# Where the weights begin in their tiles: 144 bytes in, not 192 and 0

## The chip, the cores and the metric

The kernel runs on one core of one Trainium2 chip. The metric is the device time of one execution in microseconds. Before the change it is 1110.81 us, the median of three runs (1109.86 to 1111.26).

## What is computed

One decoder layer on 512 tokens of width 1024, in float32: a feed-forward network (FFN), a token mixer, a second FFN, each with an RMS norm before it and behind it and added back to the tokens. Cut to what the change touches:

```
D_MODEL = 1024; SEQ = 512
D_FF = ((8 * D_MODEL // 3 + 127) // 128) * 128        # 2816

def swiglu(x, w_gate, w_up, w_down):
    return (jax.nn.silu(x @ w_gate) * (x @ w_up)) @ w_down

h = rms_norm(x, ffn1_pre[l])
x = x + 0.5 * rms_norm(swiglu(h, ffn1_w_gate[l], ffn1_w_up[l], ffn1_w_down[l]), ffn1_post[l])
h = rms_norm(x, mix_pre[l])
y = token_mixer(h, w_in[l], ...)
x = x + rms_norm(y, mix_post[l])
h = rms_norm(x, ffn2_pre[l])
x = x + 0.5 * rms_norm(swiglu(h, ffn2_w_gate[l], ffn2_w_up[l], ffn2_w_down[l]), ffn2_post[l])
```

The change concerns `x @ w_gate` and `x @ w_up` of both FFNs.

## The kernel before

**Three matmuls for one product.** Every float32 operand is split into a rounded high half (`fp32r`) and the rest, the low half. ScalarE writes the high half (a copy that rounds, line 384), VectorE the low half (a subtraction, line 391). `mm3` (lines 413 to 415) then multiplies high by high, high by low and low by high, and adds the three in PSUM. With weights on the left they are the stationary operand: each of the three matmuls has its own load of 128 columns of weights, and the tokens, transposed (`xh`, `xl`), are the moving operand. In the profile's names `pb_F<-xh_t,whi` is a matmul that moves `xh` past the weights `whi`.

**The weights' tiles.** `wpair` takes a tile `whi` and a tile `wlo`, each [128, 1088] in float32, three buffers of each. The pair of a split uses 1024 of the 1088 columns, from column `shift` on: byte 4 x `shift` of the tile on every partition. `wsplit` takes such a pair and fills it.

**Two ways of multiplying gate and up.** A *unit* is 128 columns of one of the two weight matrices: 8 weight tiles of 128 x 128 (one for each 128 of the 1024 rows), so 24 matmuls, each of 512 columns of tokens. At the start of each FFN, when only half of the tokens are normalised, four units are multiplied in two halves: 24 matmuls of 256 columns on the first half of the tokens, and 24 later on the second. Of the four the first three take their weights from `wpair`; the fourth has its weights in four other buffers (`wslots`, tag `SP`). Units that are not halved, and these three before the change, have `shift` 0.

Most of the columns are not done by units but by *block products* (`strassen`): the product of a block of two rows and two columns (gate and up together, two column blocks of 128 each) is formed from 7 products instead of 8. Each of the 7 is 4 weight tiles by 2 column halves, 3 matmuls each: 24 matmuls of 256 columns. Its weights, often a sum or a difference of raw weight blocks, are split by `block`, which has a `shift` of `SHIFT` = 48 columns, 192 bytes. One call of `strassen` (a *pair*: 7 products, 168 matmuls) covers 256 columns of gate and of up. The first FFN has 9 such calls (`p` from 2 to 10), the second 10 (`p` from 1 to 10); the rest of the 11 are units.

In the first FFN each call also carries VectorE work for later: sums and differences on the down weights (`weight_sums`, `early_sums`, `down_sums`, line 762), which go through HBM. At the beginning of each FFN sums on the tokens (`token_sums`) ride along as well.

**The order.** The order of the instructions on TensorE, ScalarE and VectorE is written out as a list of numbers (`ORDER`) and laid on the program at the end. DMAs are issued by SyncE. PSUM banks have the names `pb_S`, `pb_T`, `pb_V`, `pb_F`.

**Elsewhere in the mixer** a projection (`proj_T`) multiplies weights from `wsplit` with shift 0 by halves of the tokens too, 256 columns a matmul. The diff doesn't touch it.

Of the kernel before, what the change touches and what calls it, by code (L numbers as in the profile page):

```python
# [22 lines left out]
P = 128  # L23
D = 1024
S = 512
KT = D // P
# [268 lines left out]
            8: ["of"] * 2 + ["V"] * 2, 9: ["KB"] * 4}  # L295
STEPS = (2, 2, 2), (4, 2)
EARLY = 5
SHIFT = 48
HOLD_TAGS = ["W"] * 2 + ["Q"] * 4 + ["KA"] * 2 + ["V"] * 2 + ["CB", "ring"]
PS_BUFS = dict(S=3, T=2, V=1, F=2)  # L300
PS_TAGS = [t for t in PS_BUFS for _ in range(PS_BUFS[t])]
# [7 lines left out]
class Layer:  # L309
# [264 lines left out]
    def ffn(self, n, wg, wu, wd, post, finish, xsrc, tags, nps, aside=None):  # L574
# [7 lines left out]
        raws = {}  # L582
        first = {}

        def unit(m, f, slots=False):
            w = {"g": wg, "u": wu}[m]
            if self.pre_split:
                return self.pre_split.pop(0)
            if f % 2 == 0:
                raws[m] = self.raw(w[:, f * P:(f + 2) * P].rearrange("(k p) f -> p k f", p=P), [KT, 2 * P])  # L590
            src = raws[m][:, :, (f % 2) * P:(f % 2 + 1) * P]
            if slots:
                return self.wslots(src, "SP", (self.last_cast, self.last_update) if n else None)
            return self.ktiles(self.wsplit(src, [KT, P]))

        def mms(w, b, lo, hi):
            c = slice(lo, hi)
            for k in range(KT):
                self.mm3(b[:, c], w[0][k], w[1][k], self.xh[k][:, c], self.xl[k][:, c], lo + k == 0, k == KT - 1, lo > 0)
# [12 lines left out]
        def block(src):  # L612

            return self.wsplit(src, [4, 2 * P], None, SHIFT)

# [68 lines left out]

        todo = [(m, f) for f in range(NF) for m in "gu"]
        for tag, (m, f) in zip(tags, todo):
            w = unit(m, f, len(first) == 3)
            b = self.bank(tag)
            first[m, f] = w, b
            mms(w, b, 0, 2 * P)  # L690
            if len(first) in (2, 3) and self.pending:
                self.pending.pop(0)()
# [5 lines left out]
        def classical(f, act):  # L698
            bs = []
            for m in "gu":  # L700
                if (m, f) in first:
                    w, b = first[m, f]
                    mms(w, b, 2 * P, S)
                else:
                    w = unit(m, f)
                    b = self.bank()
                    mms(w, b, 0, S)
                bs.append(b)
            nc.scalar.activation(act, bs[0], AF.Silu)
            nc.vector.tensor_mul(act, act, bs[1])  # L710
            g = f - 1 + n
            if g == 0:
                sums.extend(self.token_sums())
            if 0 <= g < len(STEPS[n]):
                with self.behind(self.last_rest):
                    for _ in range(STEPS[n][g]):
                        sums.pop(0)()

        c = slice(0, H), slice(H, S)
        for p in range(NF // 2):  # L720
# [26 lines left out]
            hi, lo = [self.slot(tags["E"].pop(0), F32R) for _ in range(2)]  # L747
# [1021 lines left out]
    def run(self, out):  # L1769
        nc, a = self.nc, self.a  # L1770
        self.xdram = self.tc.dram_tile([S, D], F32, name="xdram")
        self.x2dram = self.tc.dram_tile([S, D], F32, name="x2dram")
        self.tdram = self.tc.dram_tile([NF // 2, P, 4, S], F32, name="tdram")
        self.odram = self.tc.dram_tile([NF // 2, P, S], F32, name="odram")
        self.x = [self.slot("x") for _ in range(2 * NT)]

        def lx(t):
            for h in range(2):
                nc.sync.dma_start(self.x[2 * t + h], a["x"][0][t * P:(t + 1) * P, h * S:(h + 1) * S])

        ET = mybir.EngineType
        w1 = {"g": a["ffn1_w_gate"][0], "u": a["ffn1_w_up"][0]}
        self.pre_raw = {n: self.tile(self.pool, [P, KT, 2 * P], F32, "raw", "raw", 3) for n in "gu"}

        def lw(n, i, k0=0, k1=KT):
            c = slice(i * P, (i + 1) * P)
            nc.sync.dma_start(self.pre_raw[n][:, k0:k1, c],
                              w1[n][k0 * P:k1 * P, c].rearrange("(k p) f -> p k f", p=P))

        lx(0)  # L1790
        lx(1)
        self.new_xT()
        idle = self.bank("V")

        def keep_busy(n):

            for i in range(n):
                nc.tensor.transpose(idle[:, (i % 4) * P:(i % 4 + 1) * P], self.ident, self.ident)

        with nullcontext() if ORDER else self.tc.manual_schedule(engines={ET.Activation, ET.DVE, ET.PE}):  # L1800
            keep_busy(BUSY[0])
            g = self.row_spread(a["ffn1_pre"][0], "FF")
            keep_busy(BUSY[1])
            junk = self.pre_raw["g"].rearrange("p k f -> p (k f)")[:, 0:S // 2].bitcast(BF16)
            sq = self.meansq(self.x[0], S, 1.0, junk)
            lw("g", 0, 0, 4)
            lw("g", 0, 4, KT)
            lx(2)
            lw("u", 0)
            lx(3)  # L1810
            lw("g", 1)
            lw("u", 1)
            sq0 = [sq, self.meansq(self.x[1], S)]
            sq1 = self.squares(1)
            r0 = self.rstd(sq0)
            scale0, transpose0, cast0, rest0, _ = self.norm_steps(0, g, OPEN[0])
            scale1, transpose1, cast1, rest1, _ = self.norm_steps(1, g, OPEN[1])
            hi, lo = self.wpair([KT, P])
            src = self.pre_raw["g"][:, :, 0:P]

            def whi(k):
                nc.scalar.copy(hi[:, k:k + 4], src[:, k:k + 4])

            def wlo(k):
                nc.vector.tensor_sub(lo[:, k:k + 4], src[:, k:k + 4], hi[:, k:k + 4].bitcast(F32))

            for h in range(2):
                scale0(h, r0)
                transpose0(h)
            keep_busy(BUSY[2])  # L1830
            r1 = self.rstd(sq1)
            cast0(0)
            scale1(0, r1)
            transpose1(0)
            rest0(0)
            whi(0)
            cast0(1)
            scale1(1, r1)
            keep_busy(BUSY[3])
            transpose1(1)  # L1840
            wlo(0)
            cast1(0)
            rest1(0)
            keep_busy(BUSY[4])
            whi(4)
            rest0(1)
            wlo(4)
            cast1(1)
            rest1(1)
            self.pre_split = [self.ktiles(w) for w in ((hi, lo), self.wsplit(self.pre_raw["u"][:, :, 0:P], [KT, P]))]  # L1850
            sq2 = self.squares(2)
            t2 = self.norm_T(2, g, OPEN[2], sq2, whole=True)
            self.pre_split.append(self.ktiles(self.wsplit(self.pre_raw["g"][:, :, P:2 * P], [KT, P])))
            sq3 = self.squares(3)
            r3 = self.rstd(sq3)
            self.pre_split.append(self.wslots(self.pre_raw["u"][:, :, P:2 * P], "SP"))
            t3 = self.norm_T(3, g, OPEN[3], r=r3, whole=True)
        self.pending = [t2, t3]

        def boundary(post, pre, store, tags=None, whole=False):  # L1860
            def load():
                return self.gains((post, pre))

            def finish(t, gain, r=None):
                if store is not None:
                    for h in range(2):
                        nc.sync.dma_start(store[t * P:(t + 1) * P, h * S:(h + 1) * S], self.x[2 * t + h])
                if pre is not None:
                    if t == 0:
                        self.new_xT()  # L1870
                    self.pending.append(self.norm_T(t, gain, tags[t], r=r, whole=whole))
            return load, finish

        self.ffn(0, a["ffn1_w_gate"][0], a["ffn1_w_up"][0], a["ffn1_w_down"][0],
                 *boundary(a["ffn1_post"][0], a["mix_pre"][0], self.xdram, AFTER_FFN), a["x"][0], "TTSV", 6, self.distances)
        self.mixer(*boundary(a["mix_post"][0], a["ffn2_pre"][0], self.x2dram, AFTER_MIX, True))
        self.ffn(1, a["ffn2_w_gate"][0], a["ffn2_w_up"][0], a["ffn2_w_down"][0],
                 *boundary(a["ffn2_post"][0], None, out), self.x2dram, "TTFS", 3)
# [31 lines left out]
```

## Time and profile before

| | |
|---|---|
| median of three runs | 1110.81 us (1109.86 to 1111.26) |
| the profiled execution | 1109.86 us, its span 1107.8 us |
| granted TensorE clock, mean | 0.999 |
| TensorE matmuls busy | 1098.6 us (99%), 7070 matmuls |
| weight loads busy | 996.2 us (90%) |
| VectorE busy | 915.5 us (83%) |
| ScalarE busy | 654.2 us (59%) |
| block products, first FFN | 59.4 to 237.4 us |
| block products, second FFN | 799.1 to 996.5 us |

How it is read: a matmul's drawn duration is that of its way through the array, in which the next ones already follow. What a matmul costs in a dense stretch is the distance from its start to the next one's start. The timeline gives starts (first column, us from the begin of the span) and durations (second column, us); weight loads have a row of engines of their own, `PEld`. The windows view gives, for a stretch, the busy time of each engine and the count of its instructions.

### The profile page before, as it was taken

How to read it: one execution, taken by the hardware profiler on the slowest of the kernel's cores; microseconds unless marked ns; L12 is line 12 of the kernel's file. 1: busy time of each engine (PE TensorE's matmuls, PEld its weight loads, DVE VectorE, ACT ScalarE, POOL GpSimd, SP SyncE). 2: the span in 40 equal slices, each digit the busy share in tenths (PEclk: the TensorE clock that was granted, in tenths of full speed). 3: DMA queues.
4: the chain of work that ended last, by engine and by line, in shares of the span. 5: the costliest groups of instructions: out<-in, count | busy, mean ns of one | idle time of the engine just before them, and what ended most of it. 6: DMA issues, size and time to landing. Idle time of an engine off the chain costs nothing.

```text
span 1107.8 us, 18832 instructions
## 1 busy us (share of the span) xinstructions
PE 1098.6 (99%) x7070; PEld 996.2 (90%) x7070; DVE 915.5 (83%) x1569; ACT 654.2 (59%) x1185; POOL 79.1 (7%) x112
## 2 busy tenths in 40 slices
PE   9999999999999999999999999999999999999997
PEld 7899999998889988888888998888999999998886
DVE  7799999988787878987666687977898888979674
ACT  6455555566564778787565625645565555558562
POOL 1000000000012022443000000001000000000001
PEclk9999999999999999999999999999999999999999
DMA  9967775788964562202567768683324434267862
GB/s 293 308 199 245 225 228 181 222 289 281 317 203 119 165 168 86 84 22 62 169 217 252 236 181 294 220 292 105 103 89 129 129 122 130 92 196 232 294 221 83
DMA packets 153951, 207.36 MB, mean 187 GB/s; under 512 B 19938, under 2 KB 98562, under 8 KB 153604
## 3 DMA queue, kind: packets, MB, share of 16 engines
q1 hardware_dynamic: 153856, 206.16, 57.5%
q8 instruction: 55, 0.90, 0.3%
q14 instruction: 36, 0.29, 0.1%
q10 hardware_dynamic: 4, 0.00, 0.0%
HBM read 166.76 MB, written 39.37 MB: 186 GB/s over the span
## 4 chain that ended last, share of the span: by engine, by line
PE 92%; DVE 3%; DMA 2%; ACT 1%; issue 1%; POOL 0%; SPq 0%; DVEq 0%; POOLq 0%; ACTq 0%
PE pb_F L413 12%; PE pb_F L415 12%; PE pb_F L414 11%; PE pb_S L415 8%; PE pb_S L413 8%; PE pb_S L414 8%; PE pb_T L415 6%; PE pb_T L413 6%; PE pb_T L414 6%; PE pb_V L413 3%; PE pb_V L415 3%; PE pb_V L414 3%; PE pb_V L1344 2%; PE pb_T L1329 2%; PE pb_S L1063 1%; PE pb_S L1064 1%
## 5 line engine op out<-in xcount | busy, mean ns | idle before, releaser
L384 ACT CAST whi<-raw 128x1024 fp32r<-128x1024 f32 (+1 forms) x213 | 217.5, 1023 | 238.2 <-issue 70.2
L391 DVE TENSOR_TENSOR wlo<-raw,whi 128x1024 fp32r<-128x1024 f32 (+1 forms) x213 | 252.5, 1188 | 91.5 <-ACT whi L384 87.2
L413 PE MATMUL pb_F<-xh_t,whi 128*128 128x512 f32 (+1 forms) x392 | 141.7, 363 | 0.1
L415 PE MATMUL pb_F<-xh_t,wlo 128*128 128x512 f32 (+1 forms) x392 | 140.9, 362 | 0.2 <-DVE wlo L391 0.2
L414 PE MATMUL pb_F<-xl_t,whi 128*128 128x512 f32 (+1 forms) x392 | 140.5, 360 | 0.0
L384 ACT CAST whi<-tmp_t 128x1024 fp32r<-128x1024 f32 x58 | 60.8, 1049 | 55.9 <-PE pb_S L414 22.2
L391 DVE TENSOR_TENSOR wlo<-tmp_t,whi 128x1024 fp32r<-128x1024 f32 x58 | 70.9, 1222 | 16.9 <-ACT whi L384 16.6
L415 PEld LDWEIGHTS pb_F<-xh_t,wlo 128*128 128x128 f32 x392 | 73.9, 188 | 9.5 <-DVE wlo L391 0.6
L413 PEld LDWEIGHTS pb_F<-xh_t,whi 128*128 128x128 f32 x392 | 73.9, 188 | 9.5 <-issue 0.3
L414 PEld LDWEIGHTS pb_F<-xl_t,whi 128*128 128x128 f32 x392 | 73.9, 189 | 8.9
L413 PE MATMUL pb_S<-xh_t,whi 128*128 128x256 f32 (+1 forms) x232 | 66.9, 288 | 0.0
L415 PE MATMUL pb_S<-xh_t,wlo 128*128 128x256 f32 (+1 forms) x232 | 66.7, 288 | 0.0
L414 PE MATMUL pb_S<-xl_t,whi 128*128 128x256 f32 (+1 forms) x232 | 66.6, 287 | 0.0
L1320 POOL TENSOR_SCALAR SP_s<-SP_s,st_t 128x384 f32<-128x384 f32 (+2 forms) x48 | 49.6, 1051 | 100.0 <-DVE wlo L391 50.5
L435 POOL TENSOR_TENSOR rs_t<-rs_t,mhalf_t 128x1 f32<-128x1 f32 x24 | 15.6, 648 | 532.2 <-DVE rs_t L431 531.7
L413 PE MATMUL pb_T<-xh_t,whi 128*128 128x256 f32 x184 | 51.2, 283 | 0.6 <-DVE xl_t L496 0.6
L415 PE MATMUL pb_T<-xh_t,wlo 128*128 128x256 f32 x184 | 51.6, 283 | 0.0
L414 PE MATMUL pb_T<-xl_t,whi 128*128 128x256 f32 x184 | 51.0, 281 | 0.0
L391 DVE TENSOR_TENSOR PT_s<-pb_T,PT_s 128x512 fp32r<-128x512 f32 (+1 forms) x72 | 39.7, 559 | 6.1 <-ACT PT_s L384 5.4
L1069 DVE CUSTOM_DVE_ANT_0 SP_s<-pb_S,W_s 128x128 f32<-128x128 f32 (+2 forms) x92 | 38.6, 443 | 7.1 <-PE pb_S L1064 4.7
L415 PEld LDWEIGHTS pb_S<-xh_t,wlo 128*128 128x128 f32 x232 | 43.7, 188 | 0.6
L414 PEld LDWEIGHTS pb_S<-xl_t,whi 128*128 128x128 f32 x232 | 43.6, 188 | 0.6
(858 smaller groups left out, 3458.6 us busy)
## 6 DMA issues: line engine op xcount, KB each, us to landing
raw<-in_ffn_w_up_dram SPq DMA_DIRECT2D x40, 512.0 KB, 4.5
raw<-in_ffn_w_gate_dram SPq DMA_DIRECT2D x39, 512.0 KB, 4.9
raw<-in_w_in_dram SPq DMA_DIRECT2D x18, 1024.0 KB, 5.6
raw<-in_ffn_w_down_dram SPq DMA_DIRECT2D x14, 1024.0 KB, 5.7
raw<-tdram SPq DMA_DIRECT2D x14, 1024.0 KB, 5.2
NN_s<-in_ffn_w_down_dram SPq DMA_DIRECT2D x22, 512.0 KB, 4.6
tdram<-NN_s SPq DMA_DIRECT2D x22, 512.0 KB, 3.8
odram<-ring_s SPq DMA_DIRECT2D x38, 128.0 KB, 3.5
```

The costliest lines, as they stand in the source:

```text
L384: self.last_cast = self.nc.scalar.copy(dsthi, src).ins
L391: self.last_rest = self.nc.vector.tensor_sub(dstlo, src, dsthi.bitcast(F32)).ins
L413: mm(out, lhi, rhi, start=start, stop=False, skip_group_check=skip)
L414: mm(out, lhi, rlo, start=False, stop=False, skip_group_check=skip)
L415: mm(out, llo, rhi, start=False, stop=stop, skip_group_check=skip)
L435: nc.gpsimd.tensor_tensor(out=r, in0=v, in1=self.mhalf, op=OP.pow)
L1063: mm(out, q[:, qc], ka[:, kc], start=True, stop=False)
L1064: mm(out, q[:, qc], kb[half][:, kc], start=False, stop=True)
L1069: nc.vector.tensor_tensor_reduce(p, s, w, -1.0, FLOOR, OP.add, OP.min, st_m)
L1320: nc.gpsimd.tensor_scalar(pp, pp, st[:, 1, t:t + 1], None, op0=OP.mult)
L1329: nc.tensor.transpose(b[:, o + (t - kk) * P:o + (t - kk + 1) * P], pt[pn][:, po + kk * P:po + (kk + 1) * P], self.ident)
L1344: self.nc.tensor.matmul(out[:, kk * P:S], v, pp, start=first and kk == 0 and pi == 0, stop=False, skip_group_check=True)
```

## The change

The first byte of the weights in their tiles becomes 144 for all block products (192 before), and 144 for the three halved units of each FFN whose weights lie in `whi` and `wlo` (0 before). Unhalved units, the projections of the mixer and the down products keep theirs. The tiles, their sizes and their places stay as they are.

```
-SHIFT = 48
+SHIFT = 36
...
-        def unit(m, f, slots=False):
+        def unit(m, f, slots=False, halves=False):
...
-            return self.ktiles(self.wsplit(src, [KT, P]))
+            return self.ktiles(self.wsplit(src, [KT, P], None, SHIFT if halves else 0))
...
-            w = unit(m, f, len(first) == 3)
+            w = unit(m, f, len(first) == 3, True)
...
-            hi, lo = self.wpair([KT, P])
+            hi, lo = self.wpair([KT, P], SHIFT)
...
-            self.pre_split = [self.ktiles(w) for w in ((hi, lo), self.wsplit(self.pre_raw["u"][:, :, 0:P], [KT, P]))]
+            self.pre_split = [self.ktiles(w) for w in ((hi, lo), self.wsplit(self.pre_raw["u"][:, :, 0:P], [KT, P], None, SHIFT))]
...
-            self.pre_split.append(self.ktiles(self.wsplit(self.pre_raw["g"][:, :, P:2 * P], [KT, P])))
+            self.pre_split.append(self.ktiles(self.wsplit(self.pre_raw["g"][:, :, P:2 * P], [KT, P], None, SHIFT)))
```

`block(src)`, unchanged, is `self.wsplit(src, [4, 2 * P], None, SHIFT)`.

## The prediction

> **What bounds the kernel now.** I read the page first: which engine is busy, and what the chain that ended last is made of.
>
> ```profile
> span 1107.8 us, 18832 instructions
> ...
> PE 1098.6 (99%) x7070; PEld 996.2 (90%) x7070; DVE 915.5 (83%) x1569; ACT 654.2 (59%) x1185; POOL 79.1 (7%) x112
> ...
> PE 92%; DVE 3%; DMA 2%; ACT 1%; issue 1%; POOL 0%; SPq 0%; DVEq 0%; POOLq 0%; ACTq 0%
> ```
>
> TensorE is busy for 99% of the span, and 92% of the chain is matmuls. So the time is a count of matmuls times the distance from one start to the next (the pitch). The mean duration that the groups show does not help: a matmul of 256 columns is drawn 0.28 us long while the next starts 0.12 us later. The pitch has to be taken from the timeline, as the distance between two starts with their count.
>
> The change touches the block products (products of a block recursion, 7 to a pair of column blocks, 24 matmuls of 256 columns each). One pair is 168 matmuls; here are the first matmul of a pair and of the pair behind it, in the first and in the second FFN:
>
> ```profile
> 59.40 0.28 PE L413 MATMUL pb_T<-xh_t,whi 128*128 128x256 f32 x1
> 79.18 0.28 PE L413 MATMUL pb_S<-xh_t,whi 128*128 128x256 f32 x1
> 858.03 0.28 PE L413 MATMUL pb_S<-xh_t,whi 128*128 128x256 f32 x1
> 877.82 0.28 PE L413 MATMUL pb_V<-xh_t,whi 128*128 128x256 f32 x1
> ```
>
> 19.78 and 19.79 us for 168 matmuls: 117.8 ns in both FFNs, with no gap. There are 9 such pairs in the first FFN (59.4 to 237.4 us) and 10 in the second (799.1 to 996.5 us): 1512 and 1680 matmuls, 3192 in all, about 376 us of the span. One nanosecond of pitch there is 3.2 us, 0.29%.
>
> Does the pitch hang on the address at all? The trace has the same matmul with weights that begin at the tile's begin: a projection of the mixer, which the change leaves alone (72 matmuls of 256 columns in a row, from 358.02 to 366.66), and one of the gate and up units, which it does move (24 matmuls, 793.36 to 796.24).
>
> ```profile
> 358.02 0.28 PE L413 MATMUL pb_F<-xh_t,whi 128*128 128x256 f32 x1
> 366.66 0.28 PE L413 MATMUL pb_V<-xh_t,SP_s 128*128 128x256 f32 x1
> 793.36 0.28 PE L413 MATMUL pb_F<-xh_t,whi 128*128 128x256 f32 x1
> 796.24 0.28 PE L413 MATMUL pb_S<-xh_t,SP_s 128*128 128x256 f32 x1
> ```
>
> 8.64 / 72 and 2.88 / 24 are both 120.0 ns. So weights that begin 192 bytes in run at 117.8, those that begin at 0 at 120.0: 2.2 ns apart for the same shape. And 117.8 is not the best that 192 bytes have shown. These rows are the start of the second FFN's block products:
>
> ```profile
> 799.12 0.28 PE L413 MATMUL pb_V<-xh_t,whi 128*128 128x256 f32 x1
> 812.72 0.28 PE L413 MATMUL pb_T<-NN_s,whi 128*128 128x256 f32 x1
> ...
> 813.40 0.28 PE L413 MATMUL pb_T<-PT_s,whi 128*128 128x256 f32 x1
> 813.52 0.39 PE L414 MATMUL pb_T<-CB_s,whi 128*128 128x256 f32 x1
> 813.75 0.28 PE L415 MATMUL pb_T<-PT_s,wlo 128*128 128x256 f32 x1
> 813.87 0.28 PE L413 MATMUL pb_T<-PT_s,whi 128*128 128x256 f32 x1
> ```
>
> 799.12 to 812.72 are 5 products, 120 matmuls, 13.60 us: 113.3 ns. Same offset, same shape. At 813.52 one matmul lasts 0.23 us instead of 0.113 before the next can start, and from then on the pitch is 117.8 to the end of the stretch. The weights' offset sets which pitches are possible; the phase in which TensorE enters sets which of them it keeps.
>
> What the two have to do with each other shows on the queue of weight loads, here behind that stall:
>
> ```profile
> 813.75 0.19 PEld L413 LDWEIGHTS pb_T<-PT_s,whi 128*128 128x128 f32 x1
> 813.87 0.19 PEld L414 LDWEIGHTS pb_T<-CB_s,whi 128*128 128x128 f32 x1
> 813.99 0.19 PEld L415 LDWEIGHTS pb_T<-PT_s,wlo 128*128 128x128 f32 x1
> ```
>
> The load of the next weights starts with the matmul before it and runs all along it (0.19 us against a pitch of 0.118). Both read SBUF at once. What such a matmul costs without the load in its way comes from twice the columns, with one load for each matmul and weights that are not shifted:
>
> ```profile
> 1079.79 0.39 PE L415 MATMUL pb_V<-whi,W_s 128*128 128x512 f32 x1
> 1080.47 0.39 PE L415 MATMUL pb_S<-whi,CB_s 128*128 128x512 f32 x1
> ```
>
> 0.68 / 3 = 226.7 ns, so 256 more columns cost 106.7 ns over the 120.0 at offset 0. The rest of the pitch, which doesn't grow with the columns, is 13.3 ns at offset 0, 11.1 at 192 in most of the stretch, 6.7 in the fast piece.
>
> **The change part by part.** It removes and adds no instruction; the built programs have the same rows in the same order on all five engines, the waits included. It moves the first byte of weights of the block products from 192 to 144, and that of six units (three in each FFN) from 0 to 144. What the writers of these tiles pay (ScalarE's rounding copy, VectorE's subtraction) I take as unchanged: the address is no other shape, and no row shows it to matter.
>
> No row has weights 144 bytes in. The bounds:
>
> - From above, 120.0 ns, the worst that any long stretch of this shape holds.
> - From below, the pitch of transposes of 128 columns, where a weight load per matmul is all that is left to wait for: the four of the row below take 0.60 us with 0.27 for one, and from 10.25 to 11.23 there are nine distances: 109 ns.
>
> ```profile
> 10.25 0.27 PE L1798 MATMUL pb_V<-ident_t 128*128 128x128 f32 x1
> ...
> 11.23 0.60 PE L1798 MATMUL pb_V<-ident_t 128*128 128x128 f32 x4
> ```
>
> Between them lie 117.8 and 113.3. I take 113.3: the fast piece shows that a weight address that is not the moving operand's own residue can give it, and over 3192 matmuls a new relation between the two is likelier to land on one of the shown values than on a bound. That is a choice, not a reading, and the range keeps both ends.
>
> The Trainium skill, SBUF — State Buffer, section "Who interferes with whom", gives TensorE two independent read ports, one for the moving operand and one for weight loads, and says that "PE and ACT never wait on anyone". By that rule no offset can matter and the sum would be zero, 1110.8 us; the trace disagrees already with 120.0 against 117.8.
>
> Sum for 113.3, second FFN: 126 of its 1680 matmuls have that pitch already (120 up to 812.72, six more up to 813.40), 1554 gain 117.8 - 113.3 = 4.45 ns: 6.9 us. Does anything stop it? A pair would take 168 x 113.3 = 19.04 us instead of 19.79, and the other engines' work must fit.
>
> ```profile
> core 0: us, PE busy (x) PEld busy (x) DVE busy (x) ACT busy (x) POOL busy (x), PEclk, DMA share, GB/s
> 59.40:237.40 178.00, 178.00 (x1513) 178.00 (x1512) 171.43 (x220) 99.11 (x136) 0.00 (x0) 1.00 0.69 221
> 158.30:178.10 19.80, 19.80 (x170) 19.80 (x169) 19.50 (x26) 10.88 (x15) 0.00 (x0) 1.00 0.67 206
> 217.70:237.40 19.70, 19.70 (x170) 19.70 (x169) 14.97 (x21) 11.29 (x16) 0.00 (x0) 1.00 0.74 238
> 818.40:838.20 19.80, 19.80 (x170) 19.80 (x170) 19.09 (x24) 11.29 (x16) 0.00 (x0) 1.00 0.40 125
> 858.00:877.80 19.80, 19.80 (x170) 19.80 (x169) 17.72 (x22) 10.99 (x15) 0.00 (x0) 1.00 0.38 121
> ```
>
> In a pair of the second FFN VectorE is busy for 17.72 of 19.80 us: 19.04 still holds it (the one pair at 818.4 with 19.09 loses about 0.05). In the first FFN it does not. A pair there has 19.50 us of VectorE work in 19.80, because the sums on the down weights ride along (26 instructions in the row against 22), and TensorE's third matmul of each triple waits for VectorE's low half of the weights. VectorE's idle time of the whole stretch is 178.00 - 171.43 = 6.57 us, of which the last pair has 4.73; the eight before it have 1.84 us, 0.23 a pair. A faster TensorE runs into that: of 0.75 us a pair it can keep some 0.2. I take 1.6 us for the eight pairs and 0.75 for the last, 2.4 us of the 6.7 that the pitch alone would bring. The stalls at VectorE are what is late next. That it happens shows in the fast piece: the stall at 813.52 is the matmul that reads CB_s, which VectorE finishes only at 813.46:
>
> ```profile
> 812.78 0.68 DVE L391 TENSOR_TENSOR CB_s<-V_s,PT_s 128x512 fp32r<-128x512 f32 x1
> ```
>
> The six units: 48 matmuls of 256 columns each, 288, at most 120.0 - 113.3 = 6.67 ns each: 1.9 us. In the second FFN they are back to back (0.96 us); in the first their matmuls alternate with those of an unmoved unit and with waits for loads, and I count half: 1.5 us together.
>
> Sum: 6.9 + 2.4 + 1.5 = 10.8 us. The profiled execution took 1109.86 us (span 1107.8 and 2.1 around it), the fastest of the three runs, 0.95 below their median of 1110.81. 1109.86 - 10.8 = 1099.1; against the median, 1100.0 us. For this case alone the range is 1096 to 1104: how much of VectorE's idle time is used (0 to 3 us), and the units (0 to 1.9).
>
> **The rivals.** A 0.2% difference, 2.2 us, is about what a measurement of this kernel can tell from no change.
>
> *Slower: 144 bytes are like 0.* In the built program the weights' tiles and the moving operands begin at the same remainder of 128 bytes. 144 is 16 more than a multiple of 128, and 192 is 64 more. If nearness to the moving operand's own residue is what costs, 144 sits next to offset 0 and the block products go to 120.0 ns. Everything then lies on the chain, nothing hides it: 3066 matmuls by 2.22 and the 126 fast ones by 6.67 give 6.8 + 0.8 = 7.6 us, 1118.4 us; the units stay at 120.0. For it: 0 is the nearer of the two shown offsets in that sense. Against it: nothing shows that the cost falls steadily from 0 to 64. It decides as soon as the pitch is above 118.5 (0.7 ns by 3192 is 2.2 us).
>
> *No change.* The pitch stays at 117.8 as in 19 pairs less one piece, or the offsets that are not 0 are all alike. Then only the units gain, 288 x 2.22 = 0.6 us: 1110.2 us. For it speaks that 117.8 came back after the stall at 813.52 and was never left again. By the rule of the Trainium skill quoted above (SBUF — State Buffer, "Who interferes with whom") the time would come out here too.
>
> *Much faster: the conflict goes away.* The pitch falls to the bound of 109.1. Second FFN: 1680 x 8.7 less 0.6 for what is fast already, 14.0 us; first FFN still held by VectorE, 1.84 and 1.46 for the last pair, 3.3 us; units 288 x 10.9, three quarters of it, 2.3 us: 19.6 us, 1091.2 us. No stretch of this shape comes near it.
>
> *Between 114 and 117 ns.* 2 ns less would be 3.4 us in the second FFN, about 2 in the first, under 1 in the units: 1104 to 1107 us.
>
> **How the numbers follow.** Forecast (113.3): 0.38. Between 114 and 117: 0.10. Near 109: 0.09. Together faster, 0.57. No change: 0.18. Slower: 0.25, of which 0.20 up to 120.0 and 0.05 beyond it. The predicted time is that of the forecast, 1100.0. The range goes up to the slower rival, 1118.5, and down to 1093, which leaves out most of the 109 case and what lies beyond 120.0, about 0.13.
>
> **What would show it.** Right: the distance between the first matmuls of two pairs in the second FFN is 19.04 us; in the first FFN a pair takes about 19.5 us, with single matmuls near 0.2 us apart behind VectorE's low halves, and VectorE's busy share there is over 99%; the units run at 113.3 while the mixer's projection (its rows at 358 us) stays at 120.0. Wrong: the pair at 20.16 us (the offset is like 0), or at 19.79 (nothing but the units moves). What would make the time wrong although the pitch is right: TensorE stalls for VectorE that throw it from 113.3 to 117.8, as at 813.52, and then most of the second FFN's gain is lost as well.

## The result: 0.6% slower, and the profile after

The changed kernel takes 1114.8 us (median of five runs, 1113.86 to 1117.79), the kernel before in the same comparison 1109.86 us (median of five). The ratio is 1.0059, interval [1.0033, 1.0085]: slower by 0.6%. The forecast was 1100.0 us. The profiled execution of the changed kernel took 1113.86 us, its span 1111.8 us, 4.0 us above the span of before.

The head of the profile page (span, then each engine's busy time, share of the span and count of instructions):

```profile
span 1111.8 us, 18832 instructions
PE 1103.0 (99%) x7070; PEld 1001.2 (90%) x7070; DVE 915.6 (82%) x1569; ACT 654.2 (59%) x1185; POOL 78.9 (7%) x112
```

The counts are those of before, VectorE (915.6 us against 915.5) and ScalarE (654.2 both times) work as long as before, and the mean granted clock is 0.999 both times. So the writers of the shifted tiles pay nothing that shows, as assumed. Only TensorE and its weight loads are 4.4 and 5.0 us longer. The timeline says where. These are starts of pairs of block products in the kernel after (first column: start in us; 168 matmuls from one row to the next), two neighbouring distances in the first FFN, one in the second:

```profile
59.63 0.28 PE L413 MATMUL pb_T<-xh_t,whi 128*128 128x256 f32 x1
79.77 0.28 PE L413 MATMUL pb_S<-xh_t,whi 128*128 128x256 f32 x1
99.93 0.28 PE L413 MATMUL pb_T<-xh_t,whi 128*128 128x256 f32 x1
...
861.42 0.28 PE L413 MATMUL pb_S<-xh_t,whi 128*128 128x256 f32 x1
881.30 0.28 PE L413 MATMUL pb_V<-xh_t,whi 128*128 128x256 f32 x1
```

20.16 us for 168 in the first FFN: 120.0 ns. 19.88 us in the second: 118.3 ns. Before it was 117.8 in both. The same offset now has two pitches, one in each FFN, and neither is the 113.3 that was forecast. The projection of the mixer, which the change leaves alone, is the control. Its 72 matmuls took 8.64 us before:

```profile
361.62 0.28 PE L413 MATMUL pb_F<-xh_t,whi 128*128 128x256 f32 x1
...
370.26 0.28 PE L413 MATMUL pb_V<-xh_t,SP_s 128*128 128x256 f32 x1
```

8.64 us again. The ends of the two stretches of block products are the first matmul of 512 columns behind them. Here is this row of the first and the second FFN, of before:

```profile
237.47 0.40 PE L413 MATMUL pb_F<-whi,Q_s 128*128 128x512 f32 x1
996.54 0.40 PE L413 MATMUL pb_F<-whi,Q_s 128*128 128x512 f32 x1
```

and of after:

```profile
241.05 0.40 PE L413 MATMUL pb_F<-whi,Q_s 128*128 128x512 f32 x1
...
801.78 0.28 PE L413 MATMUL pb_V<-xh_t,whi 128*128 128x256 f32 x1
...
1000.58 0.39 PE L413 MATMUL pb_F<-whi,Q_s 128*128 128x512 f32 x1
```

| stretch | before, us | after, us | difference |
|---|---|---|---|
| up to the first block product | 59.40 | 59.63 | +0.23 |
| block products, first FFN | 178.07 | 181.42 | +3.35 |
| between the two | 561.65 | 560.73 | -0.92 |
| block products, second FFN | 197.42 | 198.80 | +1.38 |
| behind them | 111.26 | 111.22 | -0.04 |

The sum is 4.0 us, the whole difference of the spans. The first FFN's part is 1512 matmuls by 2.22 ns, 3.36 us. The second's is 1554 by 0.55 ns and the 126 that were fast before by 5.0, 1.5 us, less 0.11 us for the stall at 813.52 that is gone. The middle holds the mixer, where TensorE waits for other engines: 0.4 of its 0.92 us lie at one place, the wait for VectorE's low half that ends at 395.35 us in before. No run shows that the change has to do with it. With the same lag from the first FFN the kernel blocks_only below took 561.58 us for this stretch, and blocks64, whose first FFN takes as long as before, 561.18. So 0.9 us is about what this stretch varies from run to run, and what is the change's own are the two lines of the block products, 4.7 us; the medians are 4.9 us apart.

### The profile page after: what moved, and what is told of

Read it like the earlier page. It is cut to its first block, busy times and chain, and to the rows that moved or that the text cites. A ratio compares the mean times of both kernels' runs of the same rounds, so it can differ in the third digit from the quotient of the medians.

```text
span 1111.8 us, 18832 instructions
## 1 busy us (share of the span) xinstructions
PE 1103.0 (99%) x7070; PEld 1001.2 (90%) x7070; DVE 915.6 (82%) x1569; ACT 654.2 (59%) x1185; POOL 78.9 (7%) x112
## 4 chain that ended last, share of the span: by engine, by line
PE 95%; DVE 2%; DMA 1%; ACT 1%; POOL 1%; issue 0%; SPq 0%; POOLq 0%; DVEq 0%; ACTq 0%
PE pb_F L413 12%; PE pb_F L415 12%; PE pb_F L414 12%; PE pb_S L415 8%; PE pb_S L413 8%; PE pb_S L414 8%; PE pb_T L413 6%; PE pb_T L415 6%; PE pb_T L414 6%; PE pb_V L414 3%; PE pb_V L413 3%; PE pb_V L415 3%; PE pb_V L1344 2%; PE pb_T L1329 2%; PE pb_S L1063 1%; PE pb_S L1064 1%
## 5 line engine op out<-in xcount | busy, mean ns | idle before, releaser
L415 PE MATMUL pb_F<-xh_t,wlo 128*128 128x512 f32 (+1 forms) x392 | 141.1, 362 | 0.0
L415 PEld LDWEIGHTS pb_F<-xh_t,wlo 128*128 128x128 f32 x392 | 74.0, 189 | 9.2 <-DVE wlo L391 0.3
L415 PE MATMUL pb_S<-xh_t,wlo 128*128 128x256 f32 (+1 forms) x232 | 67.3, 290 | 0.0
L415 PE MATMUL pb_T<-xh_t,wlo 128*128 128x256 f32 x184 | 52.0, 285 | 0.0
L415 PEld LDWEIGHTS pb_S<-xh_t,wlo 128*128 128x128 f32 x232 | 44.0, 189 | 0.6
L413 PEld LDWEIGHTS pb_S<-xh_t,whi 128*128 128x128 f32 x232 | 43.9, 189 | 0.6
```

What stands on the lines that cost most here:

```text
L413: mm(out, lhi, rhi, start=start, stop=False, skip_group_check=skip)
L415: mm(out, llo, rhi, start=False, stop=stop, skip_group_check=skip)
```

## The experiments

Shifts in the diffs are columns of 4 bytes: 36 is 144 bytes, 48 is 192. The expectations name theories by letter. In those of blocks_only and units_only, A holds that the block products alone cost the time, B that the shifted units do. In those of the sweeps, A holds that the byte offset alone sets the pitch (A1: its remainder by 128 does), C that only the phase at which TensorE enters a stretch sets it. All kernels here compute the whole layer; each is compared with the kernel before on the same chip.

### Which part of the change costs

*blocks_only* has the new offset in the block products and leaves the units at 0:

```
-SHIFT = 48
+SHIFT = 36
```

> The block products at 144, the six halved units at 0 as before. Theory A (the pitch of the block products is all that counts): a pair of the second FFN takes 168 x 118.3 = 19.88 us or 168 x 120.0 = 20.16 us, the same in the first FFN, and the time is 2 to 7.6 us over the kernel before, about 1114. Theory B (the shifted units are what costs): the block products run at 117.8 as before, and the time is within 0.2% of before, 1110. If the units only set the phase in which the block products are entered, the first FFN may run at 118.3 here instead of the 120.0 of the changed kernel: 1512 x 1.67 ns = 2.5 us less than that.

Measured: 1114.98 us, ratio 1.0046 [1.0032, 1.0060], with 120.0 ns in the first FFN and 118.3 in the second, as in the changed kernel.

*units_only* is the other half: the changed kernel with its block products back at 192 bytes.

```
 SHIFT = 36
+BLOCKS = 48
...
-            return self.wsplit(src, [4, 2 * P], None, SHIFT)
+            return self.wsplit(src, [4, 2 * P], None, BLOCKS)
```

> The six halved units at 144, the block products at 192 as before. Theory A: the units gain at most 1.7 to 2.2 ns on 288 matmuls, under 0.7 us, and the block products keep 117.8 (or 113.3 in a piece, which would show as up to 6.9 us less in an FFN): 1109 to 1110 us. Theory B: about 1114 us as the changed kernel.

Measured: 1110.31 us, ratio 1.0004 [0.9995, 1.0013]. Block products as in the kernel before, the fast piece at the start of the second FFN included. The units are worth nothing that can be measured; the loss is the block products' alone.

### Other offsets, one for each pair

In these kernels every call of `strassen` has an offset of its own, so that one trace shows 19 of them. *sweep_up* goes up from 0 in steps of 16 bytes, *sweep_down* has the same list backwards, so that each offset is seen at another place and behind another one. The one exception is 144 bytes, the tenth of the nineteen: in both it is the first call of the second FFN, where the changed kernel had 118.3 ns as well. *sweep_fine* goes between them.

```
-SHIFT = 48
+SHIFTS = {2: 0, 3: 4, 4: 8, ...}, {1: 36, 2: 40, ...}
...
+        shift = [0]
+
         def strassen(p):
+            shift[0] = SHIFTS[n][p]
...
-            return self.wsplit(src, [4, 2 * P], None, SHIFT)
+            return self.wsplit(src, [4, 2 * P], None, shift[0])
```

> One look: every call of the block products has an offset of its own, rising through the program: 0, 16, 32 ... 128 bytes in the first FFN's nine calls, 144, 160 ... 256, then 8 and 24 bytes in the second's ten. Theory A1 (the offset counts modulo 128, with the moving operand's remainder): the pair at 16 bytes runs like 144 (118.3 or 120.0), 64 like 192 (117.8 or 113.3), 0, 128 and 256 at 120.0. Theory A2 (the offset counts modulo 256 or not in such a way): 16 and 144, 64 and 192 differ. Theory C (only the phase at entry counts, the offset hardly): the pitch stays where it was when the offset changes from call to call.

> One look: the same nineteen offsets in falling order, so that each is entered from the other side and in the other FFN. Theory A1: each offset gives a pitch out of the same small set as in the rising order. Theory C: the pitches follow the order and the FFN, not the offset.

> One look: nineteen more offsets, one a call: 64, 68, 72, 76, 88, 104, 120, 136, 152 bytes in the first FFN, 4, 12, 20, 28, 36, 40, 44, 52, 56, 60 in the second. If only multiples of 16 bytes matter, 64 to 76 run alike at 113.3 and 4, 12 alike at 120.0. If every 4 bytes count (8 and 24 bytes gave 115.5 and 121.9, between them 16 gave 118.3), the pitch goes up and down within 16 bytes, and some offset may lie below 113.3.

The times are 1112.76, 1112.74 and 1110.57 us, one run each; what counts is the pitch of each pair. Two distances show how they were read. In sweep_up (64 bytes from the first row on, 80 from the second, 96 from the third):

```profile
139.57 0.28 PE L413 MATMUL pb_T<-xh_t,whi 128*128 128x256 f32 x1
158.61 0.28 PE L413 MATMUL pb_S<-xh_t,whi 128*128 128x256 f32 x1
178.57 0.28 PE L413 MATMUL pb_T<-xh_t,whi 128*128 128x256 f32 x1
```

19.04 us at 64 bytes (113.3 ns) and 19.96 at 80 (118.8). In sweep_down, where 80 stands in the second FFN and 64 follows it:

```profile
880.51 0.28 PE L413 MATMUL pb_V<-xh_t,whi 128*128 128x256 f32 x1
900.68 0.28 PE L413 MATMUL pb_S<-xh_t,whi 128*128 128x256 f32 x1
```

20.17 us at 80 bytes: 120.0, not 118.8. All offsets, pitch in ns (sweep_up and sweep_down agree except where two numbers stand):

| bytes | ns | bytes | ns | bytes | ns |
|---|---|---|---|---|---|
| 0 | 120.0 | 96 | 118.7 | 192 | 117.8 |
| 8 | 115.5 | 112 | 120.0 | 208 | 116.7 |
| 16 | 118.3 | 128 | 118.7 | 224 | 116.7 |
| 24 | 121.9 | 144 | 118.3 | 240 | 120.0 |
| 32 | 118.3 | 160 | 120.0 | 256 | 120.0 |
| 48 | 117.8 | 176 | 118.1 | | |
| 64 | 113.3 | 80 | 118.8 / 120.0 | | |

and in sweep_fine: 4: 118.3, 12: 116.7, 20: 120.0, 28: 116.7, 36: 120.0, 40: 119.2, 44: 117.8, 52: 113.3, 56: 117.8, 60: 119.5, 64: 117.8, 68: 118.3, 72: 118.3, 76: 113.3, 88: 113.3, 104: 120.0, 120: 119.4, 136: 118.0, 152: 117.8.

Four things follow. The pitch hangs on the offset, in steps as small as 4 bytes, and follows no slope. 0 and 128, 32 and 160 differ in both sweeps, so it isn't the remainder by 128 alone; 0 and 256 agree. Some values come again and again: 113.3, 116.7, 117.8, 118.3 and 120.0 make up most of the table. And an offset does not always have the same one: 80 has 118.8 and 120.0, 64 has 113.3 in two kernels and 117.8 in a third. (So 64 and 192, at 113.3 and 117.8 in the sweeps, are no proof of a difference: each of the two has shown both values.) Neither A nor C holds alone.

### The address itself, or the distance to the moving operand

*moved64* moves every tile behind it 64 bytes further, weights and tokens alike, by a tile that nothing uses:

```
+        self.pool.tile([P, 16], F32, name="gap_t", tag="gap", bufs=1)
```

> The kernel before with 64 unused bytes ahead of all tiles: every SBUF address goes up by 64, the block products' weights stay 192 bytes into their tiles. If the distance between weights and moving operand counts, the pitches are those of before (117.8, and 113.3 in the first five products of the second FFN), about 1110 us. If the weights' own address counts, they are those of 256 bytes: 120.0 and about 1117.5 us.

Measured: 1111.47 us (one run), and the pitches of before in every place: 117.8, and 113.3 in the first five products of the second FFN. By their own address the weights lay where 256 bytes put them in the sweeps, and would have run at 120.0 like these; they did not. So the address alone is not what counts, but where the weights lie in relation to something that moved along. The moving operand, which TensorE reads at the same time, is the likely one. A kernel that moves it alone was not run for these products; for the down products all76 and both76 below do that, and their pitch changes with it.

### One good offset for all block products

64 bytes had shown 113.3 ns in the sweeps. *blocks64* uses it for the block products (`SHIFT = 16` in the kernel before), *blocks64_units64* for the halved units too (the same in the changed kernel).

> Block products at 64 bytes throughout, units at 0. In both sweeps a call at 64 bytes ran at 113.3 ns. If the offset keeps that pitch from any entry: second FFN 1680 matmuls at 113.3, 6.9 us less than before. If VectorE caps the first FFN as my prediction had it (19.5 us of work a pair), the first FFN saves 2.4 us and the time is 1100.8; if VectorE's work fits into 19.04 us a pair, the first FFN saves 6.7 us and the time is 1096.5. If a stall throws 64 bytes into 117.8 as it did with 192, the time is near 1110 again.

> As the kernel with the block products at 64 bytes, with the six halved units at 64 too. If the units gain what the block products do, up to 6.7 ns on at most 288 matmuls: 0.5 to 1.9 us less than without. If, as with 144, their stage hides it: no difference.

Measured: 1110.61 us, ratio 1.0014 [0.9998, 1.0030], and 1109.74 us, ratio 1.0003 [0.9990, 1.0016]. In both every pair ran at 117.8, not at 113.3. 64 bytes have two pitches, and here both stretches began at the slower one and stayed there.

*blocks52* (`SHIFT = 13`) and *blocks76* (`SHIFT = 19`) take two other offsets that had shown 113.3:

> Block products at 52 bytes throughout, units at 0. In the fine sweep 52 was entered from 117.8 and went over to 113.3 within its first product (mean 114.3). If it draws the pitch to 113.3 from every entry: 12 to 14 us less than before, 1096 to 1098, or about 1101 if VectorE's work caps the first FFN. If it too has a second pitch of 117.8 or more that some entries lock: near 1110.

> Block products at 76 bytes throughout, units at 0. In the fine sweep 76 ran at 113.3, entered from 118.3. Same alternatives as at 52 bytes: 1096 to 1098 if it holds 113.3 from every entry and VectorE keeps up, about 1101 if VectorE caps the first FFN, near 1110 or above if another pitch locks.

blocks52: ratio 0.9993 [0.9968, 1.0018], but its twelve runs fall into two groups, nine from 1105.4 to 1107.2 us and three from 1116.4 to 1116.8. The profiled one is of the first group and has 120.0 ns in the first FFN and 113.3 in the second. The three others lie 10.9 us above the median of these nine, which 120.0 in the second FFN as well would give (1680 x 6.67 = 11.2 us); they were not profiled, so this is inferred.

blocks76: 1099.46 us, ratio 0.9912 [0.9886, 0.9937]. A pair of the second FFN and one of the first (168 matmuls each):

```profile
874.50 0.28 PE L413 MATMUL pb_F<-NN_s,whi 128*128 128x256 f32 x1
893.54 0.28 PE L413 MATMUL pb_S<-NN_s,whi 128*128 128x256 f32 x1
...
156.37 0.28 PE L413 MATMUL pb_S<-xh_t,whi 128*128 128x256 f32 x1
175.78 0.28 PE L413 MATMUL pb_T<-xh_t,whi 128*128 128x256 f32 x1
```

and the same stretches in the windows (columns as in the prediction's table of windows), with the last pair of the first FFN in the middle row:

```profile
156.37:175.78 19.41, 19.41 (x171) 19.21 (x169) 19.38 (x26) 10.90 (x15) 0.00 (x0) 1.00 0.63 197
214.68:234.00 19.32, 19.32 (x171) 19.15 (x169) 16.40 (x23) 11.31 (x16) 0.00 (x0) 1.00 0.74 245
874.50:893.54 19.04, 19.04 (x170) 19.04 (x169) 17.55 (x22) 10.99 (x15) 0.00 (x0) 1.00 0.39 125
```

19.04 us in the second FFN, 113.3 ns. In the first FFN 19.41 us, and VectorE, the third busy column, works 19.38 of them: it is the bound there. The stall itself, VectorE's low half and the matmul that reads it, with the matmuls around it:

```profile
174.90 1.22 DVE L391 TENSOR_TENSOR wlo<-raw,whi 128x1024 fp32r<-128x1024 f32 x1
```

```profile
175.89 0.28 PE L414 MATMUL pb_T<-xl_t,whi 128*128 128x256 f32 x1
176.17 0.38 PE L415 MATMUL pb_T<-xh_t,wlo 128*128 128x256 f32 x1
176.39 0.28 PE L413 MATMUL pb_T<-xh_t,whi 128*128 128x256 f32 x1
```

The low half is done at 176.12, and the matmul that needs it starts at 176.17, 0.28 us behind the one before it. Unlike at 813.52 us in the kernel before, TensorE returns to 113.3 behind each such stall here. In its block products this kernel is the one that the prediction described, at another offset; its halved units are at 0.

### What picks one of an offset's pitches

*enter144* leads into long stretches of 144 bytes from other offsets, to see whether the place or what stands ahead decides:

```
+SHIFTS = {2: 0, 3: 4, 4: 36, ... 10: 36}, {1: 0, 2: 36, ... 10: 36}
```

> One look. The block products at 144 as in the changed kernel, but entered differently: in the first FFN the first call is at 0 bytes, the second at 16 (118.3 in both sweeps), the other seven at 144; in the second FFN the first call is at 0 (120.0), the other nine at 144. If the phase at entry decides between the two pitches of 144, they change places: the first FFN's calls at 144 run at 118.3 (19.88 us a pair) instead of 120.0, the second FFN's at 120.0 (20.16) instead of 118.3. If something else of the two FFNs decides (their moving operands, their other work), the first stays at 120.0, the second at 118.3.

Measured: 1114.84 us (one run); 144 ran at 120.0 in the first FFN (behind 16 bytes) and at 118.3 in the second (behind 0). The two did not change places as that expectation had it. This fits either answer: the FFN may decide, or an entry behind 16 bytes may lead to 120.0 and one behind 0 to 118.3. The kernel entries144 below tells them apart.

*enter192* has 192 bytes everywhere but in the second call of each FFN, which has 76 (`SHIFTS = {2: 48, 3: 19, 4: 48, ...}, {1: 48, 2: 19, 3: 48, ...}`):

> One look. The kernel before (192 bytes) but for one call in each FFN, the second, which is at 76 bytes (113.3 in the fine sweep, entered from 118.3). If 192 bytes keep the phase in which they are entered, the calls behind it run at 113.3, the last 7 of the first FFN and the last 8 of the second with the two at 76: 17 x 0.75 = 12.7 us less, about 1097, or, where VectorE's 19.5 us a pair hold in the first FFN, about 1102. If 192 falls back by itself, only the two calls gain: 1108.5.

Measured: 1100.42 us (one run), 9.4 us below the median of the kernel before although 17 of its 19 calls have the same 192 bytes. Rows of the first FFN:

```profile
98.41 0.28 PE L413 MATMUL pb_T<-xh_t,whi 128*128 128x256 f32 x1
117.45 0.28 PE L413 MATMUL pb_S<-xh_t,whi 128*128 128x256 f32 x1
...
175.38 0.28 PE L413 MATMUL pb_T<-xh_t,whi 128*128 128x256 f32 x1
194.81 0.28 PE L413 MATMUL pb_S<-xh_t,whi 128*128 128x256 f32 x1
```

98.41 to 117.45 is the pair behind 76 bytes, at 192 bytes: 19.04 us, 113.3 ns, where the kernel before has 117.8. The pairs behind it take 19.0 to 19.5 (VectorE's stalls), and from the last row on they are back at 117.8. In between, stalls throw 192 bytes both ways. Here a third matmul of a triple (L415), which reads the low half of the weights, twice takes 0.22 us before the next can start:

```profile
153.25 0.39 PE L415 MATMUL pb_S<-xh_t,wlo 128*128 128x256 f32 x1
153.47 0.28 PE L413 MATMUL pb_S<-xh_t,whi 128*128 128x256 f32 x1
155.94 0.28 PE L413 MATMUL pb_S<-xh_t,whi 128*128 128x256 f32 x1
156.24 0.38 PE L415 MATMUL pb_S<-xh_t,wlo 128*128 128x256 f32 x1
156.46 0.28 PE L413 MATMUL pb_S<-xh_t,whi 128*128 128x256 f32 x1
172.44 0.28 PE L413 MATMUL pb_F<-xh_t,whi 128*128 128x256 f32 x1
```

Up to 153.25 the pitch is 113.3. Behind that stall 21 matmuls take 2.47 us (153.47 to 155.94), 117.6 ns; behind the one at 156.24 it is 113.3 again, 141 matmuls in 15.98 us (156.46 to 172.44). The next pair repeats this, and in the one after it the second stall, at 195.10, does not bring 113.3 back. In the second FFN all calls behind the 76 stay at 113.3 to the end. So 192 bytes can run at either pitch; what runs ahead picks, and so does a stall.

*entries144* puts 144 bytes behind seven offsets, some in both FFNs, in turn (`SHIFTS = {2: 0, 3: 36, 4: 16, 5: 36, 6: 19, 7: 36, 8: 3, 9: 36, 10: 40}, ...`):

> One look. Every second call of the block products is at 144 bytes, the calls between at 0, 64, 76, 12, 160 in the first FFN and 16, 32, 76, 12, 160 in the second. If the FFN decides (its moving operands' places, its other work), all four calls at 144 of the first FFN run at 120.0 and all five of the second at 118.3. If the entry decides, both pitches occur in both FFNs, and the same predecessor (76, 12) gives the same pitch in both.

Measured: 1111.13 us (one run). Rows of the first FFN (76 bytes from the first row on, then 144, 12, 144, 160) and of the second (the same):

```profile
139.06 0.28 PE L413 MATMUL pb_T<-xh_t,whi 128*128 128x256 f32 x1
158.11 0.28 PE L413 MATMUL pb_S<-xh_t,whi 128*128 128x256 f32 x1
178.26 0.28 PE L413 MATMUL pb_T<-xh_t,whi 128*128 128x256 f32 x1
197.87 0.28 PE L413 MATMUL pb_S<-xh_t,whi 128*128 128x256 f32 x1
217.47 0.28 PE L413 MATMUL pb_T<-xh_t,whi 128*128 128x256 f32 x1
...
879.63 0.28 PE L413 MATMUL pb_V<-xh_t,whi 128*128 128x256 f32 x1
898.69 0.28 PE L413 MATMUL pb_S<-xh_t,whi 128*128 128x256 f32 x1
918.84 0.28 PE L413 MATMUL pb_V<-xh_t,whi 128*128 128x256 f32 x1
938.44 0.28 PE L413 MATMUL pb_S<-xh_t,whi 128*128 128x256 f32 x1
958.05 0.28 PE L413 MATMUL pb_V<-xh_t,whi 128*128 128x256 f32 x1
```

| 144 bytes behind | pitch ahead, ns | first FFN, ns | second FFN, ns |
|---|---|---|---|
| 0 | 120.0 | 118.3 | 118.3 (enter144) |
| 12 | 116.7 | 116.7 | 116.7 |
| 16 | 118.3 | 120.0 (enter144) | 120.0 |
| 64 | 113.3 | 120.0 | |
| 76 | 113.3 | 120.0 | 120.0 |
| 32 | 118.3 | | 120.0 |
| 160 | 120.0 | | 116.7 |

Behind 76 it is 20.15 us in both FFNs, behind 12 it is 19.60 and 19.61. Every predecessor that was tried in both FFNs gave the same pitch in both. So it isn't the FFN; it is what ran ahead. I call what the stretch ahead hands over the phase; no row shows the phase itself. 144 bytes have three pitches, 116.7, 118.3 and 120.0, and none of seven entries gave 113.3. What the pitch ahead is does not tell it by itself: behind 0 and behind 160, both at 120.0, 144 came out differently.

### What else the offset can be used for

*all76* has 76 bytes as the default of `wpair` and `wsplit`, so that the 512-column units, the projections and the down products, where the split weights are the moving operand, are shifted as well:

```
-    def wpair(self, shape, shift=0):
+    def wpair(self, shape, shift=SHIFT):
...
-    def wsplit(self, src, shape, behind=None, shift=0):
+    def wsplit(self, src, shape, behind=None, shift=SHIFT):
```

> All weights split into whi and wlo begin 76 bytes in: block products, units (halved and of 512 columns), the mixer's projections, and the down products, where the weights are the moving operand. Block products as in the kernel with 76 bytes alone (1099.5 us). If 76 bytes take 6.7 ns off every matmul with weights from whi and wlo: 288 + 144 matmuls of 256 columns (2.9 us) and 1008 of 512 columns in units (6.7 us) more, and the 984 of 512 columns with the weights moving, whose distance is -76, go either way: about 1090 us without them. If only matmuls of 256 columns, where load and matmul are equally long, have such pitches: 1096.6 us. If the wider ones lose: above 1099.5.

Measured: 1102.54 us, ratio 0.9930 [0.9917, 0.9942]: faster than before, slower than blocks76. With 512 columns a matmul the shift costs. The first matmuls of two neighbouring units (24 matmuls) of the first FFN, in the kernel before:

```profile
47.16 0.39 PE L413 MATMUL pb_F<-xh_t,whi 128*128 128x512 f32 x1
...
52.60 0.39 PE L413 MATMUL pb_S<-xh_t,whi 128*128 128x512 f32 x1
```

and in all76:

```profile
49.23 0.39 PE L413 MATMUL pb_S<-xh_t,whi 128*128 128x512 f32 x1
...
54.83 0.39 PE L413 MATMUL pb_S<-xh_t,whi 128*128 128x512 f32 x1
```

5.44 us against 5.60: 226.7 ns at 0 bytes, 233.3 at 76 (single distances of 231 and 236). Down products went from 226.7 to 228 to 230.

*both76* keeps all76 and gives the down products' weights 180 bytes (`self.wsplit(src, [2, S], None, 45)` and the like):

> As before, but the weights of the down products (moving operand) begin 180 bytes in, so that the distance from moving to stationary operand is 76 modulo 256 there too. If the distance modulo 256 is what counts in both roles, the down products run at the pitch that the units of 512 columns have at 76: 984 matmuls, up to 6.7 ns each, up to 6.6 us less than with 76 bytes everywhere, or no change if the 512-column pitch does not hang on it.

Measured: 1110.9 us, ratio 1.0009 [0.9997, 1.0021]: the down products took about 238 ns, and the gain was gone. In its profiled run, the longest of eleven (1114.73 us), the first FFN fell from 113.3 to 120.0: the matmul at 133.56 us took 0.22 us before the next could start, and from there to the end of the stretch no piece is at 113.3 again. So 76 bytes are not safe against every stall.

*cols256_76* uses 76 bytes only where the moving operand has 256 columns: the changed kernel with `SHIFT = 19`, and the halves of the mixer's projection:

```
-SHIFT = 36
+SHIFT = 19
...
-            w = [[v[:, k] for k in range(KT)] for v in self.wsplit(src, [KT, P])]
+            w = [[v[:, k] for k in range(KT)] for v in self.wsplit(src, [KT, P], None, SHIFT if part else 0)]
```

> 76 bytes for the block products, the six halved units and the three halved projections of the mixer; everything of 512 columns begins at 0. If the pitch follows the distance, 288 + 144 matmuls more run at 113.3 instead of 120.0, at most 2.9 us less than the kernel with 76 bytes in the block products alone (1099.5): 1096.6 to 1099. The two FFNs' 512-column units stay at 226.7. If the halved units' stage is bound by its loads and norms rather than by its matmuls, nothing more than 1099.5.

Measured: 1097.03 us (1096.71 to 1099.02), ratio 0.9889 [0.9872, 0.9905]: faster than both kernels of this case, 1.1% below the one before. The mixer's projection (60 matmuls between the rows) and 168 matmuls of block products of the second FFN:

```profile
353.97 0.28 PE L413 MATMUL pb_F<-xh_t,whi 128*128 128x256 f32 x1
...
360.77 0.28 PE L413 MATMUL pb_S<-xh_t,whi 128*128 128x256 f32 x1
...
912.69 0.28 PE L413 MATMUL pb_T<-NN_s,whi 128*128 128x256 f32 x1
...
931.73 0.28 PE L413 MATMUL pb_F<-NN_s,whi 128*128 128x256 f32 x1
```

6.80 / 60 and 19.04 / 168: 113.3 ns in both, against 120.0 and 117.8 before.

## Why the prediction was wrong, and where it was right

**The step that failed** is the choice of 113.3 ns for 144 bytes between the bounds of 109 and 120.0. It gave 10.8 us of gain; the block products in fact took 120.0 ns in the first FFN and 118.3 in the second and cost 4.7 us (3.35 and 1.38). The argument for the choice was that a new relation between the two operands would land on one of the values already shown. It nearly did (120.0 was shown, 118.3 lies 0.5 from 117.8), but I took the best of the shown values for the likeliest. In the sweeps only five of the 37 offsets (52, 64, 76, 88 and, at 115.5, 8) came within 3 ns of the best; eleven lay at or above 119.5 at least once. By that count 113.3 had a small chance, and "like 192" or worse most of it. The trace of before had the two sorts of evidence in it (an offset of 192 bytes with two pitches, an offset of 0 with another) and no row at any third offset; nothing in it could tell which of them 144 would have. The upper bound was not one for the shape either: 24 bytes run at 121.9.

**The slower rival** described the first FFN to the digit: 120.0 ns, 20.16 us a pair, 1512 x 2.22 = 3.4 us. Its time, 1118.4 us, needed the second FFN to go the same way, which went to 118.3 in the profiled run. Its reason, nearness to the moving operand's residue of 128 bytes, fell: 16 bytes run at 118.3, 8 at 115.5, and 0 and 128 differ. The two slowest runs of the changed kernel, 1116.2 and 1117.8 us, fit a second FFN at 120.0 too (1680 x 1.67 = 2.8 us more); they have no profile.

**"The offset sets which pitches are possible; the phase sets which of them it keeps"** was right, and more so than the prediction used it. Enter192 shows the same 192 bytes at both pitches, entries144 shows three for 144. (Phase is a name here for what ran ahead; no row shows it.) Having said so, the prediction should have asked what the units ahead would hand over, and should have had the two FFNs as two separate throws.

**VectorE's cap in the first FFN, and the sum for 113.3**, were right in kind for the kernel that has that pitch, and one term was too small. In blocks76 a pair of the second FFN takes 19.04 us, as forecast, and the whole stretch gains the 6.9 us that were forecast (197.42 to 190.52). In the first FFN seven of nine pairs take 19.3 to 19.5 us, against "about 19.5", with stalls of about 0.2 us behind low halves and VectorE at 19.38 of 19.41 us. But the first two run at 19.05 and 19.04, and the stretch gains 4.1 us (178.07 to 173.96), not 2.4. The working let each pair do its VectorE work within that pair. The rows show that part of it can come later: the last pair holds 16.40 us of it in 23 instructions, where before it held 15.05 in 21 (217.69 to 237.47). So that 1099.46 us was measured and 1100.0 forecast is partly luck: the forecast counted 1.5 us for the units, which are at 0 in blocks76, and 1.7 us too little for the first FFN.

**The units** (1.5 us) were wrong by the same choice: at 144 bytes the matmuls of the halved units ran mostly between 115 and 121 ns, about 119 in the mean in both FFNs against just under 120 at 0 bytes, and units_only shows no gain that can be measured. At 76 bytes most of them run at 113 to 114. blocks76 and cols256_76, timed on different chips, differ by 2.4 us. In their traces 1.6 us of it lie between the two stretches of block products, where the projection and the second FFN's units are. The first FFN's units lie ahead of 60.04 us in one and of 58.92 in the other, and that begin alone goes from 59.3 to 61.3 us in kernels whose units are at 0, so their part stays open.

**The rule of two independent ports** (the Trainium skill, SBUF — State Buffer, section "Who interferes with whom") would have every kernel here at the same pitch. The runs disagree with it: 113.3 to 121.9 ns, with the count and order of instructions unchanged.

**What stays open.** What makes the values (113.3, 115.5, 116.7, 117.8, 118.3, 119.2, 120.0, 121.9 and some between) was not found, nor a rule from an offset to its values. Why 144 bytes start at 120.0 in the first FFN and at 118.3 in the second was not taken apart: units run ahead of both, 512-column ones in the first FFN and halved ones in the second, and whether the halved ones are at 144 or at 0 makes no difference (the changed kernel and blocks_only have the same two pitches). That the weight load and the matmul's own reads disturb one another would fit that the relation of the two addresses counts, but no run shows the mechanism itself.

## What to carry to other kernels

Where dense matmuls with a weight load each bound the kernel, take the pitch from the timeline (distance of starts, with their count), compare it between stretches of the same shape, and where it differs by a few per cent, try other places of the weights in their tiles: one kernel with another offset for each block shows nineteen of them in one trace. Then time the winner in its place, since one offset can have several pitches and what runs ahead, or a stall, picks among them; a value that was seen once is not a value that will be kept. And choose per shape: the offset that was best for 256 columns (76 bytes) was worse than 0 for 512.

## What was not expected of the hardware

- The pitch of one and the same matmul (256 columns, with a load of 128 x 128 weights) goes from 113.3 to 121.9 ns with the weights' offset as the only edit, and changes in steps of 4 bytes: 16 bytes 118.3, 20 bytes 120.0, 24 bytes 121.9, 28 bytes 116.7.
- It keeps its pitch over a whole stretch, up to 1680 matmuls, without drifting: 64 bytes ran at 113.3 in one call each of three kernels and at 117.8 through both FFNs of two others, 192 bytes at 117.8 or 113.3, 144 at 116.7, 118.3 or 120.0. A single stall can switch it to the slower pitch (192 bytes, at 813.52 us in the kernel before; 76 bytes, at 133.56 in both76), back to the faster one (192 bytes, at 156.24 in enter192), or not at all (76 bytes, behind each of VectorE's stalls in blocks76).
- Moving both operands by 64 bytes changed no pitch of the block products (moved64).
- This can make single runs of one program differ. Four of some eighty runs of the kernel before took 1102.2 to 1103.6 us, some 7 us below its median, which is what a second FFN at 113.3 throughout would give (6.9 us). None of those runs was profiled, so that this is their cause is inferred.
